# Splitting the weights of a two-block fp32 network with DMA transfers instead of VectorE

## The chip, the core and the metric

The kernel runs on one core of one Trainium2 chip. The metric is the device time of one execution in microseconds; the time before is the median of three runs. A profile comes from one further execution, whose own time stands beside its span below. The engines that matter are TensorE (PE in the profile, its weight loads PEld), VectorE (DVE), ScalarE (ACT), GpSimd (POOL) and SyncE (SP), which only issues transfers. Transfers can be issued from the queues of SP, ACT and POOL.

## The reference

Two transformer-like blocks run over 512 positions of width 1024, all in fp32, with one layer each.

```python
# first block
h = rmsnorm(x, attn_norm_g)
z = h @ w_in
gates = sigmoid(h @ w_gate + b_gate)
y_a, y_b, y_c = gmlp_mixer(...), pool_mixer(...), diff_attn_mixer(...)   # from columns of z
x = x + (g_a * (y_a @ proj_a) + g_b * (y_b @ proj_b) + g_c * (y_c @ proj_c)) @ w_out
x = x + conv_ffn(rmsnorm(x, ffn_norm_g), w_up, conv_w, conv_b, w_down)    # gelu(conv(gate)) * up
x = rmsnorm(x, final_norm_g)
# second block
x = x + dilated_attention_mixer(rms_norm(x, mixer_norm), attn_w_in, q_gain, k_gain, attn_w_out)
x = x + conv_ffn_2(rms_norm(x, ffn_norm), ffn_w_up, ffn_conv_w, ffn_conv_b, ffn_w_down)
```

`pool_mixer` takes moving averages over 2, 4, 8 and 16 positions. Both FFNs have 2816 hidden channels, that is 22 tiles of 128 for the gate and 22 for the up half.

## The kernel before

**Splitting.** TensorE multiplies operands of type float32r. To keep fp32 accuracy each operand is split in two: a leading part `hi`, the fp32 value rounded to float32r, and a remainder `lo`, the fp32 value less `hi`. A product is then three matmuls (`mm3`, line 97): hi·hi, hi·lo and lo·hi. This holds for activations (tiles xh and xl, ah and al, and so on) and for weights (tiles wh and wl).

**Units.** All weights pass through in 234 units (`unit`, line 151) of 128 partitions by 1024 columns, or 768 in every third unit of the two down projections. A unit is 24 matmuls of 128x512 (18 where it has 768 columns). The order is: uv (4 units), v (4), the q and k heads with the two units b0 and b1 of the pooling branch (10), the gates with the merging projections (32), the output projection `wo` (8), the first FFN's gate and up units in turn (44), its down projection `dn` (24); then the second block: q/k and v groups `n`, `vn`, `c` and `vc` (36), the output projection `wo2` (4), gate and up `vg` and `vu` (44) and the down projection `en` (24).

**A step.** The loop at line 1321 runs once for each unit, in an order written by hand; each engine executes its own instructions in program order. Step u consists of:

- `fn` (line 1323): the matmuls of unit u;
- `prep_hi(u+3)` (line 1324): ScalarE copies the loaded weights (tile wr) of unit u+3 to float32r, which makes wh;
- `prep_lo(u+2)` (line 1325): VectorE (POOL for the two units vg0 and vu0) subtracts wh from wr, which makes wl of unit u+2;
- the work that earlier steps put off (`early`);
- the loads of raw weights, issued from SP (`load`, line 161), up to six units ahead;
- `post`: the eviction of unit u's PSUM result and what follows from it; some of this is put off to a later step;
- `fills`: other work pinned to this step, such as attention scores, norms and transposes.

**Buffers.** wr has four buffers, wh four and wl three. The wl buffer of unit u+2 is that of unit u−1, so it is free once unit u−1's matmuls have ended; the same holds for the wh buffer of unit u+3.

**What POOL does.** The steps of the prediction touch these: `accumulate` (line 256) sums squares on POOL for a norm, once in each step m = 1 to 6 of the output projection (`wout_post`, line 710) and twice in each column m = 1 to 6 of the first down projection (`down1_post`, line 781). `rpow` (line 235) raises statistics to the power −0.5; it serves the norms (`r_a`, line 282; `b2_stat`, line 800), the attention (`da_n1`, line 605) and the q/k groups (`qk_norm`, line 845). `pool_win` (line 454) computes both tiles of the moving averages in the step of b1. `perm` (line 832) and `bd_prep` (line 874) copy and clear tiles at the start of the second block. In the FFNs one product of each pair of units runs on POOL (`gate1_post`, line 733, tile gl; `up2_post`, line 1150, tile act), put off to the step after its unit.

Of the kernel before, what the change touches and what calls it, by code (L numbers as in the profile page):

```python
# [23 lines left out]
F32 = mybir.dt.float32  # L24
F32R = mybir.dt.float32r
AF = mybir.ActivationFunctionType
OP = mybir.AluOpType
# [7 lines left out]
FT = 22  # L35
LA = 2
RAW = 4
WARM = 9
NSLOT = 51
NDUO = 13  # L40
# [15 lines left out]
def build(tc, a):  # L56
    nc = tc.nc
    te, ve, ac, po = nc.tensor, nc.vector, nc.scalar, nc.gpsimd
    ctx = ExitStack()
    with ctx:  # L60
        cp = ctx.enter_context(tc.tile_pool(name="cp", bufs=1))
        wp = ctx.enter_context(tc.tile_pool(name="wp", bufs=1))
# [22 lines left out]
        def f(t):  # L85
            return t.bitcast(F32)
# [15 lines left out]
        def tt(out, x, y, op, eng=None):  # L102
            (eng or ve).tensor_tensor(out, x, y, op=op)  # L103
# [41 lines left out]
        units = []  # L145
# [13 lines left out]
        raws, hls = {}, {}  # L159

        def load(j):
            if j < len(units):
                src, n = units[j][:2]
                raws[j] = wp.tile([128, 1024], F32, name="wr", tag="wr", bufs=RAW)
                nc.sync.dma_start(raws[j][:, :n], src)

        def prep_hi(j):
            if j < len(units):
                n = units[j][1]
                hi = wp.tile([128, 1024], F32R, name="wh", tag="wh", bufs=LA + 2)  # L170
                ac.activation(hi[:, :n], raws[j][:, :n], AF.Copy)  # L171
                hls[j] = hi

        def prep_lo(j):
            if j < len(units) and j in raws:
                n = units[j][1]
                lo = wp.tile([128, 1024], F32R, name="wl", tag="wl", bufs=LA + 1)
                tt(lo[:, :n], raws.pop(j)[:, :n], f(hls[j])[:, :n], OP.subtract,
                   po if names.get(j) in ON_POOL else ve)
                hls[j] = (hls[j], lo)  # L180

        def fm(out, hl, j0, n, xh, xl, k0, start, stop, t=slice(0, S)):
            hi, lo = hl
            for k in range(n):
                c = slice((j0 + k) * 128, (j0 + k + 1) * 128)
                mm3(out[:, t], hi[:, c], lo[:, c], xh[k0 + k][:, t], xl[k0 + k][:, t],
                    start and k == 0, stop and k == n - 1)
# [481 lines left out]
        for m2 in range(4):  # L669
# [6 lines left out]
            def fn(hl, m2=m2, st=st):  # L676
                for e in range(2):
                    pa, pb = acc(), acc()
                    st[e] = (pa, pb)
                    for t in range(2):  # L680
                        for y, p, o in ((YA, pa, 0), (YB, pb, 2)):
                            c = slice((4 * e + o + t) * 128, (4 * e + o + t + 1) * 128)
                            mm3(p, hl[0][:, c], hl[1][:, c], y[t][0], y[t][1], t == 0, t == 1)
# [570 lines left out]
        g0 = cp.tile([128, 8], F32, name="g0")  # L1254
        ve.memset(ones, 1.0)
        ac.activation(hb[:, :1], ones[:, :1], AF.Copy)
        raws[0] = wp.tile([128, 1024], F32, name="wr", tag="wr", bufs=RAW)
        for m in range(8):
            X[m] = slot("x")
        xs = lambda m: a["xT"][128 * m:128 * m + 128, :]  # L1260
# [6 lines left out]
        for m in (3, 5, 7):  # L1267
            nc.gpsimd.dma_start(X[m], xs(m))
        for j in range(1, RAW):
            nc.sync.dma_start(X[2 * j], xs(2 * j))  # L1270
            load(j)
            if j == 2:
                nc.sync.dma_start(prm, a["prm"])
        for i in range(WARM):
            te.matmul(warm[:, :128], ones, ones, start=True, stop=True)
        ve.memset(mh, -0.5)
        wh0 = wp.tile([128, 1024], F32R, name="wh", tag="wh", bufs=LA + 2)
        wl0 = wp.tile([128, 1024], F32R, name="wl", tag="wl", bufs=LA + 1)
        hls[0] = (wh0, wl0)
        XH[0], XL[0] = slot("xh", F32R), slot("xl", F32R)  # L1280
        p0.extend(misc() for _ in range(4))
# [15 lines left out]
        for j in range(1, LA + 1):  # L1297
            norm_in(2 * j, X[2 * j], g0[:, 2 * j:2 * j + 1], "r1")
            prep_hi(j)
            prep_lo(j)  # L1300
            norm_in(2 * j + 1, X[2 * j + 1], g0[:, 2 * j + 1:2 * j + 2], "r1")
# [17 lines left out]
        pend = []  # L1319
        loaded = RAW  # L1320
        for u_, (src, n, fn, post, defer) in enumerate(units):
            now[0] = u_
            fn(hls.pop(u_))
            prep_hi(u_ + LA + 1)
            prep_lo(u_ + LA)
            first = names.get(u_) in FIRST
            if not first:
                for fl, args in early.pop(u_, []):
                    fl(*args)
            while loaded <= u_ + LA + RAW and loaded < len(units):  # L1330
                load(loaded)
                loaded += 1
            if post is not None:
                pend.append((u_ + defer, post))
            while pend and pend[0][0] <= u_:
                pend.pop(0)[1]()
            if first:
                for fl, args in early.pop(u_, []):
                    fl(*args)
            for fl, args in fills.get(u_, []):  # L1340
                fl(*args)
        assert not pend and not early, early.keys()


# [115 lines left out]
```

## Time and profile before

| | |
|---|---|
| median of 3 runs | 1374.84 us (1374.4 to 1374.93) |
| the profiled execution's own time | 1375.68 us |
| its span, first to last instruction | 1373.8 us |
| mean granted TensorE clock | 0.999 |
| transfers | 46185 packets; 127.19 MB read from HBM |

How to read the lines that the prediction shows: in a row of the groups stand line, engine, operation, tiles written and read, shapes and count, then busy time in us and the mean of one in ns, then idle time of the engine just before them and what ended it. A row of the timeline begins with the start and the duration in us; in brackets stands how long the engine was idle before it and what released it. A row of the chain of work that ended last has the start, the length, and the engine, tile and line. A row of transfers has the issuing queue (SPq, POOLq), the count, the size of one, and the median time from its issue to its landing. A row of the windows has, for a stretch of time, the length and the busy time of PE, PEld, DVE, ACT and POOL with their instruction counts, then the granted clock, the share of time the DMA engines were busy, and GB/s.

### The profile page before, as it was taken

The page shows a single profiled execution, that of the slowest core. Times are in us where ns is not written, and L with a number is a line of the kernel's source. Part 1 is how long each engine was busy: PE and PEld are TensorE (multiplying, and loading weights), DVE is VectorE, ACT ScalarE, POOL GpSimd, SP SyncE. Part 2 cuts the span into 40 slices and gives each one's busy share as a digit, 9 for nine tenths or more (in the row PEclk, how much of TensorE's full clock was granted, in tenths as well). Part 3 has the DMA queues.
Part 4 walks back from the last instruction along what each step waited for, and adds up shares of the span by engine and source line. Part 5 has one row for each costly group of instructions (what it writes and reads, how often), then busy time and mean ns, then how long its engine had stood idle before and what let it go on. Part 6 is the DMA issues. An engine that isn't in the chain of part 4 may idle for free.

```text
span 1373.8 us, 16670 instructions
## 1 busy us (share of the span) xinstructions
PE 1363.8 (99%) x6360; PEld 1137.4 (83%) x6360; DVE 808.5 (59%) x1328; ACT 603.2 (44%) x974; POOL 248.7 (18%) x208
## 2 busy tenths in 40 slices
PE   9999999999999999999999999999989999999998
PEld 7888888888888888888888888888868888888887
DVE  6777664556555545533347667667878666665222
ACT  6547543333343333332234667645654444443110
POOL 3250111101111111101117122231341111110000
PEclk9999999999999999999999999999999999999999
DMA  7434222433333332333323342222123233223330
GB/s 256 127 101 124 77 79 90 129 116 92 106 95 92 96 104 92 91 97 100 96 92 98 104 109 63 69 85 63 62 88 97 93 93 106 93 88 107 115 110 25
DMA packets 46185, 134.62 MB, mean 98 GB/s; under 512 B 9924, under 2 KB 10639, under 8 KB 46105
## 3 DMA queue, kind: packets, MB, share of 16 engines
q1 hardware_dynamic: 45048, 131.30, 31.3%
q0 software_dynamic: 912, 2.19, 0.5%
q8 instruction: 50, 0.82, 0.2%
q14 instruction: 31, 0.25, 0.1%
q10 hardware_dynamic: 144, 0.07, 0.0%
HBM read 127.19 MB, written 2.14 MB: 94 GB/s over the span
## 4 chain that ended last, share of the span: by engine, by line
PE 98%; DVE 1%; issue 0%; ACT 0%; DMA 0%; DVEq 0%; POOLq 0%
PE acc L89 89%; PE ms L89 2%; PE cs L89 1%; PE cu L89 1%; PE qkt L885 1%; PE nu L89 1%; PE sc L89 1%; PE ns L89 1%; PE pv L89 1%; DVE xl L106 1%; PE ctr L1056 0%; PE ntr L949 0%; PE tr L583 0%; DVE y L103 0%; DMA g<-in_prm 0%
## 5 line engine op out<-in xcount | busy, mean ns | idle before, releaser
L89 PE MATMUL acc<-xh,wh 128*128 128x512 f32 x968 | 378.0, 390 | 0.0
L89 PE MATMUL acc<-xl,wh 128*128 128x512 f32 x968 | 376.8, 389 | 0.0
L89 PE MATMUL acc<-xh,wl 128*128 128x512 f32 x968 | 376.8, 389 | 0.0
L103 DVE TENSOR_TENSOR wl<-wr,wh 128x1024 fp32r<-128x1024 f32 (+2 forms) x233 | 297.3, 1276 | 127.7 <-PE acc L89 77.3
L171 ACT ACTIVATE wh<-wr 128x1024 fp32r<-128x1024 f32 (+1 forms) x233 | 242.0, 1039 | 210.9 <-PE acc L89 174.0
L89 PEld LDWEIGHTS acc<-xh,wl 128*128 128x128 f32 x968 | 181.7, 188 | 38.2
L89 PEld LDWEIGHTS acc<-xh,wh 128*128 128x128 f32 x968 | 181.7, 188 | 37.3
L89 PEld LDWEIGHTS acc<-xl,wh 128*128 128x128 f32 x968 | 181.8, 188 | 37.0
L89 PE MATMUL acc<-al,wh 128*128 128x512 f32 (+1 forms) x358 | 138.0, 385 | 0.0
L89 PE MATMUL acc<-ah,wl 128*128 128x512 f32 (+1 forms) x358 | 138.0, 385 | 0.0
L89 PE MATMUL acc<-ah,wh 128*128 128x512 f32 (+1 forms) x358 | 138.0, 385 | 0.0
L725 ACT ACTIVATE cv<-z,prm 128x512 f32<-128x512 f32 x66 | 53.7, 816 | 165.8 <-DVE z L103 165.8
L106 DVE SCALAR_TENSOR_TENSOR cv<-z,prm,cv 128x511 f32<-128x511 f32 (+1 forms) x132 | 99.5, 756 | 2.4
L89 PEld LDWEIGHTS acc<-al,wh 128*128 128x128 f32 x358 | 67.2, 188 | 13.6
L89 PEld LDWEIGHTS acc<-ah,wl 128*128 128x128 f32 x358 | 67.2, 188 | 13.5
L89 PEld LDWEIGHTS acc<-ah,wh 128*128 128x128 f32 x358 | 67.2, 188 | 13.4
L89 PE MATMUL acc<-wh,ch 128*128 128x512 f32 x192 | 75.8, 395 | 0.0
L89 PE MATMUL acc<-wl,ch 128*128 128x512 f32 x192 | 74.9, 390 | 0.0
L89 PE MATMUL acc<-wh,cl 128*128 128x512 f32 x192 | 74.8, 390 | 0.0
L103 POOL TENSOR_TENSOR gl<-cv,r2b 128x512 f32<-128x512 f32 x22 | 28.4, 1290 | 202.9 <-ACT cv L739 202.9
L103 POOL TENSOR_TENSOR act<-cv,cv 128x512 f32<-128x512 f32 x22 | 28.4, 1289 | 202.0 <-DVE cv L106 188.4
L236 POOL TENSOR_TENSOR rr<-ss,mh 128x8 f32<-128x8 f32 x24 | 38.8, 1644 | 114.1 <-DVE ss L857 114.1
(333 smaller groups left out, 1958.4 us busy)
## 6 DMA issues: line engine op xcount, KB each, us to landing
wr<-in_w_up SPq DMA_DIRECT2D x88, 512.0 KB, 3.5
wr<-in_w_dn SPq DMA_DIRECT2D x32, 512.0 KB, 3.5
wr<-in_w_g SPq DMA_DIRECT2D x24, 512.0 KB, 3.5
wr<-in_w_qkc SPq DMA_DIRECT2D x16, 512.0 KB, 3.5
wr<-in_w_o SPq DMA_DIRECT2D x12, 512.0 KB, 3.5
wr<-in_w_dn SPq DMA_DIRECT2D x16, 384.0 KB, 3.1
wr<-in_w_qkn SPq DMA_DIRECT2D x8, 512.0 KB, 3.9
wr<-in_w_vc SPq DMA_DIRECT2D x8, 512.0 KB, 3.4
```

The lines of the kernel that those rows point to most:

```text
L89: te.matmul(out, l, r, start=start, stop=stop, skip_group_check=True)
L103: (eng or ve).tensor_tensor(out, x, y, op=op)
L106: ve.scalar_tensor_tensor(out, x, s, y, op0=o0, op1=o1)
L171: ac.activation(hi[:, :n], raws[j][:, :n], AF.Copy)
L236: po.tensor_tensor(out, src, mh[:, :n], op=OP.pow)
L725: ac.activation(c, z, AF.Identity, scale=P(cw, 2 * n + j), bias=P(cb, j))
L885: te.transpose(p[:, 128 * b:128 * b + 128], qs[b][:, 128 * part:128 * part + 128], identf)
```

## The change

From index 12 of the units on (the thirteenth), no raw weights are loaded to SBUF any more. A transfer issued from POOL reads the fp32 weights from HBM and converts them to float32r as it writes wh (`cast`). ScalarE writes −wh to wl (`negate`). A second transfer from POOL reads the weights from HBM again and adds them to wl (`add`), so wl holds the weights less wh. In the loop the negation stands for unit u+2 where the VectorE subtraction stood; the add for unit u+2 and the cast for unit u+4 come at the very end of step u, behind its fills. wh has five buffers instead of four, wr three instead of four, wl three as before. The first twelve units are prepared as before.

```diff
+WH = 5
+WL = 3
+J0 = 12
         def load(j):
-            if j < len(units):
+            if j < min(J0, len(units)):
                 src, n = units[j][:2]
-                raws[j] = wp.tile([128, 1024], F32, name="wr", tag="wr", bufs=RAW)
+                raws[j] = wp.tile([128, 1024], F32, name="wr", tag="wr", bufs=3)
                 nc.sync.dma_start(raws[j][:, :n], src)
...
+        def cast(j):
+
+            if J0 <= j < len(units):
+                src, n = units[j][:2]
+                hi = wp.tile([128, 1024], F32R, name="wh", tag="wh", bufs=WH)
+                nc.gpsimd.dma_start(hi[:, :n], src)
+                hls[j] = hi
+
+        def negate(j):
+            if J0 <= j < len(units):
+                n = units[j][1]
+                lo = wp.tile([128, 1024], F32R, name="wl", tag="wl", bufs=WL)
+                ac.activation(lo[:, :n], f(hls[j])[:, :n], AF.Copy, scale=-1.0)
+                hls[j] = (hls[j], lo)
+
+        def add(j):
+
+            if J0 <= j < len(units):
+                src, n = units[j][:2]
+                nc.gpsimd.dma_start(hls[j][1][:, :n], src, accum_op=OP.add)
...
             fn(hls.pop(u_))
             prep_hi(u_ + LA + 1)
             prep_lo(u_ + LA)
+            negate(u_ + 2)
...
             for fl, args in fills.get(u_, []):
                 fl(*args)
+            add(u_ + 2)
+            cast(u_ + 4)
```

`prep_hi` and `prep_lo` get the same bound `min(J0, len(units))` as `load`, and all allocations of wh and wl use `WH` and `WL`.

More of the change, by code (lines that the diff above doesn't have):

```diff
@@ L161, in load @@
         def load(j):
-            if j < len(units):
+            if j < min(J0, len(units)):
                 src, n = units[j][:2]
-                raws[j] = wp.tile([128, 1024], F32, name="wr", tag="wr", bufs=RAW)
+                raws[j] = wp.tile([128, 1024], F32, name="wr", tag="wr", bufs=3)
                 nc.sync.dma_start(raws[j][:, :n], src)
         def prep_hi(j):
-            if j < len(units):
+            if j < min(J0, len(units)):
                 n = units[j][1]
-                hi = wp.tile([128, 1024], F32R, name="wh", tag="wh", bufs=LA + 2)
+                hi = wp.tile([128, 1024], F32R, name="wh", tag="wh", bufs=WH)
                 ac.activation(hi[:, :n], raws[j][:, :n], AF.Copy)
@@ L174, in prep_lo @@
         def prep_lo(j):
-            if j < len(units) and j in raws:
+            if j < min(J0, len(units)) and j in raws:
                 n = units[j][1]
-                lo = wp.tile([128, 1024], F32R, name="wl", tag="wl", bufs=LA + 1)
+                lo = wp.tile([128, 1024], F32R, name="wl", tag="wl", bufs=WL)
                 tt(lo[:, :n], raws.pop(j)[:, :n], f(hls[j])[:, :n], OP.subtract,
@@ L180, in prep_lo @@
                 hls[j] = (hls[j], lo)
+        def cast(j):
+            if J0 <= j < len(units):
+                src, n = units[j][:2]
+                hi = wp.tile([128, 1024], F32R, name="wh", tag="wh", bufs=WH)
+                nc.gpsimd.dma_start(hi[:, :n], src)
[3 more added lines that the diff above has]
+                n = units[j][1]
+                lo = wp.tile([128, 1024], F32R, name="wl", tag="wl", bufs=WL)
+                ac.activation(lo[:, :n], f(hls[j])[:, :n], AF.Copy, scale=-1.0)
[4 more added lines that the diff above has]
+                nc.gpsimd.dma_start(hls[j][1][:, :n], src, accum_op=OP.add)
         def fm(out, hl, j0, n, xh, xl, k0, start, stop, t=slice(0, S)):
@@ L1256, in build @@
         ac.activation(hb[:, :1], ones[:, :1], AF.Copy)
-        raws[0] = wp.tile([128, 1024], F32, name="wr", tag="wr", bufs=RAW)
+        raws[0] = wp.tile([128, 1024], F32, name="wr", tag="wr", bufs=3)
         for m in range(8):
@@ L1276, in build @@
         ve.memset(mh, -0.5)
-        wh0 = wp.tile([128, 1024], F32R, name="wh", tag="wh", bufs=LA + 2)
-        wl0 = wp.tile([128, 1024], F32R, name="wl", tag="wl", bufs=LA + 1)
+        wh0 = wp.tile([128, 1024], F32R, name="wh", tag="wh", bufs=WH)
+        wl0 = wp.tile([128, 1024], F32R, name="wl", tag="wl", bufs=WL)
         hls[0] = (wh0, wl0)
```

## The prediction

> **What bounds the kernel now.** I read first the page's busy shares and its chain, then the whole chain in order of time, then the POOL engine's timeline, since POOL receives the work.
>
> ```profile
> span 1373.8 us, 16670 instructions
> PE 1363.8 (99%) x6360; PEld 1137.4 (83%) x6360; DVE 808.5 (59%) x1328; ACT 603.2 (44%) x974; POOL 248.7 (18%) x208
> PE 98%; DVE 1%; issue 0%; ACT 0%; DMA 0%; DVEq 0%; POOLq 0%
> ...
> L103 DVE TENSOR_TENSOR wl<-wr,wh 128x1024 fp32r<-128x1024 f32 (+2 forms) x233 | 297.3, 1276 | 127.7 <-PE acc L89 77.3
> ```
>
> ```profile
> 5.93 24.02 PE ms L89 x96
> ...
> 252.98 108.84 PE acc L89 x480
> ...
> 368.19 353.63 PE acc L89 x1560
> ...
> 1026.91 342.99 PE acc L89 x1530
> ```
>
> TensorE sets the end. In the third long stretch 1560 matmuls take 353.63 us, 0.2267 us each, with no gap, so a unit of 24 matmuls lasts 5.44 us. The DVE subtraction that the change takes away (1.28 us in each unit) lies beside those 5.44 us and is nowhere in the chain. So there is next to nothing to win: the question is whether the two weight halves still arrive in time, for whatever is late now is added to a chain that has no slack.
>
> **What the change moves.** From index 12 on (222 of 234 units) one SP load, one ScalarE copy and one DVE subtraction become a POOL-issued cast, a ScalarE negation of the same size (costed as the copy: no change) and a POOL-issued add. SP loses 222 loads, DVE some 280 us that cost nothing before. POOL, 18% busy, gains 444 issues.
>
> ```profile
> wr<-in_w_up SPq DMA_DIRECT2D x88, 512.0 KB, 3.5
> ...
> wr<-in_w_dn SPq DMA_DIRECT2D x16, 384.0 KB, 3.1
> ...
> x<-in_xT SPq DMA_DIRECT2D x11, 256.0 KB, 3.8
> ...
> x<-in_xT POOLq DMA_DIRECT2D x4, 256.0 KB, 7.0
> ...
> msk<-in_msk POOLq DMA_DIRECT2D x1, 256.0 KB, 3.9
> ```
>
> ```profile
> 20.26 2.11 POOL L450 DMA_DIRECT2D pw<-in_pool_w  x4 [3.70 <-DVE pw L447]
> 22.33 0.58 POOL L495 DMA_DIRECT2D oh<-in_oh  x1
> ```
>
> An issue takes POOL 0.53 to 0.58 us (2.11 over 4; 0.58), so 444 make some 245 us: POOL goes to about 36%, harmless as a share. The order is what matters. The last two rows show that POOL issues strictly in turn: oh depends on nothing, yet it goes out only after pw, which stood waiting for DVE.
>
> The price of one add, from issue to landing, is not in this trace. Its lower bound is a plain load of the same size, 3.5 us. Its upper bound is the dearest POOL-issued 256 KB, 7.0 us, in the crowded first microseconds. Between: 512 KB against 384 KB differ by 0.4 us, so a pass over 512 KB costs 1.6 us; an add also reads what it adds to, a second pass, 3.5 + 1.6 = 5.1; POOL's 256 KB took 0.1 more than SP's. I take 5.2 us and keep 3.5 and 7.0 for the range.
>
> The step's order decides the rest. In step u the add for unit u+2 stands at the very end, behind every POOL instruction of that step. The DVE subtraction stood ahead of them, on another engine. So where a POOL instruction of step u waits for unit u's own matmuls, the add for u+2 is issued only after unit u has ended, with one unit (5.44 us) left instead of two. The added wait is (end of the last POOL instruction of step u) + 5.2 − (start of unit u+2 before).
>
> The new waits themselves are short. The add waits for ScalarE's negation, which can start when unit u−1 has ended, as the copy did; behind it on POOL stand the cast for u+4 and the next step's sums and powers, whose users (ScalarE, DVE, the statistics) have a step or more of slack. The negation waits for its cast, issued two steps earlier right behind an add; behind it on ScalarE stand the step's evictions. Each lead is about two units, 10.9 us, less the delays below, and I cost both at nothing; if a cast came later than that, the evictions would be next, and then TensorE's PSUM banks.
>
> Down projection of the first FFN: x2, then norm, squares, and two POOL sums.
>
> ```profile
> 626.66 0.69 DVE L103 TENSOR_TENSOR x<-acc,x 128x512 f32<-128x512 f32 x1 [2.80 <-PE acc L89]
> ```
>
> ```profile
> 628.71 1.34 POOL L103 TENSOR_TENSOR rfacc<-sq 128x512 f32<-128x512 f32 x1 [31.99 <-ACT sq L279]
> 630.02 2.00 POOL L103 TENSOR_TENSOR rgacc<-sq 128x512 f32<-128x512 f32 x1
> ```
>
> The unit ended about 0.2 us before x, at 626.5, so the unit after next starts at 631.9. POOL is free at 632.0; the add lands at 637.2: 5.3 us late, in six of the eight columns: 31.8 us.
>
> Output projection: one POOL sum in steps 1 to 6 of eight.
>
> ```profile
> 325.83 1.33 POOL L103 TENSOR_TENSOR r2acc<-sq 128x512 f32<-128x512 f32 x1 [75.64 <-ACT sq L279]
> ```
>
> Free at 327.16; the unit after next would start at 252.98 + 14 × 5.442 = 329.17: 3.2 us late. Once it is late the next add has that time to spare, so every second one stalls: 3 × 3.2 = 9.6 us.
>
> The pooling windows (step of b1), which put over twenty POOL instructions in one step:
>
> ```profile
> 84.96 1.04 POOL L103 TENSOR_TENSOR wsum<-zb 128x511 f32<-128x511 f32 x1 [37.61 <-DVE zb L103]
> ...
> 104.49 1.30 POOL L103 TENSOR_TENSOR pd<-win,zb 128x512 f32<-128x512 f32 x1
> ```
>
> ```profile
> 97.12 5.44 PE acc L89 x24
> ```
>
> Free at 105.79, unit due at 97.12: 13.9 us late. Next the start of the second block, where the statistics and the permuting copies stand on POOL (with the memsets and four powers ahead of the second copy):
>
> ```profile
> 727.21 1.09 POOL L835 CAST cl<-xl 128x512 fp32r<-128x512 f32 x1
> ...
> 750.11 1.59 POOL L835 CAST cl<-xl 128x512 fp32r<-128x512 f32 x1
> ```
>
> ```profile
> 722.81 10.91 PE acc L89 x48
> ...
> 734.15 16.35 PE acc L89 x72
> ```
>
> Free at 728.30, due at 722.81 + 5.46 = 728.27: 5.2 us. Free at 751.70, due at 734.15 + 10.90 = 745.05: 11.9 us (both move alike with what came before).
>
> Powers on POOL behind the statistics of a step's own result: four in the attention, five after the q/k groups, one each behind the second and third norm; the first and last of the two groups, and the two single ones, with the units they delay:
>
> ```profile
> 164.40 1.03 POOL L236 TENSOR_TENSOR or<-om,mh 128x4 f32<-128x4 f32 x1 [14.73 <-DVE om L608]
> ...
> 243.09 1.86 POOL L236 TENSOR_TENSOR or<-om,mh 128x4 f32<-128x4 f32 x1 [22.75 <-DVE om L608]
> ...
> 363.53 1.92 POOL L236 TENSOR_TENSOR r<-ms,mh 128x4 f32<-128x4 f32 x1 [9.16 <-DVE ms L285]
> ```
>
> ```profile
> 793.88 6.44 POOL L236 TENSOR_TENSOR rr<-ss,mh 128x8 f32<-128x8 f32 x4 [31.83 <-DVE ss L857]
> ...
> 942.89 6.44 POOL L236 TENSOR_TENSOR rr<-ss,mh 128x8 f32<-128x8 f32 x4 [22.37 <-DVE ss L857]
> ...
> 1022.25 1.93 POOL L236 TENSOR_TENSOR r<-ms,mh 128x4 f32<-128x4 f32 x1 [8.55 <-DVE ms L285]
> ```
>
> ```profile
> 169.92 5.46 PE acc L89 x24
> ...
> 241.63 10.92 PE acc L89 x48
> ...
> 797.43 10.91 PE acc L89 x48
> ...
> 950.84 5.47 PE acc L89 x24
> ```
>
> Attention: 165.43 + 5.2 − 169.92 = 0.7 for the first, 244.95 + 5.2 − 247.09 = 3.1 for the last; with the two between, 9.6 us for the four. Groups: 800.32 + 5.2 − 802.89 = 2.6 and 949.33 + 5.2 − 950.84 = 3.7; 14.1 for the five. The norms: 365.45 + 5.2 − 368.19 = 2.5, and 1024.18 + 5.2 − 1026.91 = 2.5.
>
> The 88 up-projection units nearly escape, as their POOL product belongs to the step before:
>
> ```profile
> 508.40 1.28 POOL L103 TENSOR_TENSOR gl<-cv,r2b 128x512 f32<-128x512 f32 x1 [9.65 <-ACT cv L739]
> ...
> 1122.90 1.29 POOL L103 TENSOR_TENSOR act<-cv,cv 128x512 f32<-128x512 f32 x1 [9.59 <-DVE cv L106]
> ```
>
> 509.68 + 5.2 = 514.9 against a due time of 368.19 + 27 × 5.442 = 515.1, and 1124.19 + 5.2 = 1129.4 against 1026.91 + 19 × 5.442 = 1130.3. No cost, but 0.2 and 0.9 us are all the cover: every tenth that an add takes over 5.4 us costs 2.2 us in the first FFN's 22 pairs.
>
> Waits: 31.8 + 9.6 + 13.9 + 5.2 + 11.9 + 9.6 + 14.1 + 2.5 + 2.5 = 101 us.
>
> **The clock** comes on top.
>
> ```profile
> 1370.00:1374.00 4.00, 0.00 (x0) 0.00 (x0) 0.35 (x1) 0.00 (x0) 0.00 (x0) 0.74 0.10 35
> ```
>
> In the last 4 us TensorE has nothing to do and the granted clock averages 0.74: half speed for some 2 of the 4, after some 2 of idling. A cold start costs 24.02 − 96 × 0.2267 = 2.3 us in the first chain row. Ten of the waits above pass 4.5 us (six columns, the pooling, the two at the second block, one group): 10 × 2.2 = 22 us. The Trainium skill, "TensorE: Matmul & The Clock Gate", section "What's actually happening", has the clock halve after an idle window of about 3.4 us and return after as long a busy one; by it each restart would cost about 1.7 us, 17 in all, and the trace's quicker fall at the end disagrees with its idle time.
>
> Costed at nothing: the third weight buffer instead of a fourth in the first units (the fourth load waits for the first buffer; cover is ScalarE's squares, and the range holds the rest). Sum: 1375.68 us (the profiled execution: 1373.8 of span and 1.9 around it, 0.8 above the median 1374.84) + 123; against the median, **1498 us**.
>
> **Rivals.** (1) *A cheap add.* If it lands like a plain load (3.5), each of 22 waits is 1.7 us shorter and most stay too short to cool the clock: 123 − 37 − 15 = 71, 1446 us. It is also the time if the converting transfer doesn't round at all: the copies are the same. (2) *A dear add, or transfers at their limit.*
>
> ```profile
> 258.00:722.00 464.00, 464.00 (x2051) 384.15 (x2050) 234.56 (x275) 168.35 (x214) 57.84 (x41) 1.00 0.33 100
> ```
>
> A plain load now keeps the DMA engines busy for 0.33 × 5.44 = 1.8 us a unit, the small ones included; about 1.7 is the load. Cast and add at three passes need 5.1 of 5.44 and fit; at four, 6.8 don't: 1.3 us more in each of the 148 units of the two gapless stretches, 192 us, 1690. An add of 7.0 us that is only late gives 1.8 × 22 + (1.6 + 0.9) × 22 = 95 more, 1593. The Trainium skill, "Collectives: The Full Stack", section "The bandwidth ceiling: the fold count and why AG ≠ RS ≠ AR", says a transfer that adds is slower for its two reads and not for the addition; by it add and cast would be three passes. No row here shows one. (3) *Not slower.* If POOL took the adds past its waiting instructions, every add would have two units, 10.9 us, and even 7.0 us would be hidden; the relief of DVE and the 1% of idle TensorE then allow at most some 5 us of gain, 1370. It decides where POOL's queue isn't in order; the pw and oh rows speak against it.
>
> **How the numbers follow.** Forecast (adds of 4.4 to 6 us, 1470 to 1560): 0.52. Cheap add: 0.15. Dear add or transfer limit: 0.30. Not slower: 0.03. Range 1440 to 1690: from the cheap add to the transfer limit, leaving out what is beyond four passes and the last rival. A measurement of this kernel can tell about 0.2%: faster by more 0.02, within 0.01, slower 0.97.
>
> **What would show it.** Right: TensorE waits for wl's DMA, none in the up-projections, about 5 us at every third unit of the first down projection, over 10 at the pooling and the second block; none in the last down projection, whose steps have no POOL work. Granted clock under 1 after those. Landing of an add about 5 us. Wrong: waits in every unit, DMA share near 1 (the limit); POOL issues of adds ahead of its sums; landings far from 5 us; or a wait for wh instead of wl, a cast that comes late.

## The result, and the profile after

The changed kernel takes 1518.84 us (median of 4 runs, 1513.77 to 1522.02) against 1374.88 us before: ratio 1.1044, 95% interval 1.1019 to 1.1069, so 144 us slower. The forecast was 1498 us in a range of 1440 to 1690. The profiled execution has a span of 1519.0 us at a mean granted clock of 0.966.

From the page of the changed kernel: span, busy times, share of the chain by engine, three groups, the POOL queue's packets, and the two kinds of transfer.

```profile
span 1519.0 us, 16761 instructions
...
PE 1408.4 (93%) x6360; PEld 1162.2 (77%) x6360; DVE 544.5 (36%) x1108; ACT 605.0 (40%) x974; POOL 538.8 (35%) x650
...
q0 software_dynamic: 64848, 230.81, 66.5%
...
PE 37%; DMA 5%; issue 4%; POOL 2%; DVE 2%; ACT 2%; POOLq 0%; DVEq 0%; ACTq 0%
...
L197 ACT ACTIVATE wl<-wh 128x1024 fp32r<-128x1024 f32 (+1 forms) x222 | 230.8, 1040 | 403.2 <-PE acc L92 129.6
...
L92 PE MATMUL acc<-ah,wl 128*128 128x512 f32 (+1 forms) x358 | 143.3, 400 | 25.5 <-DMA wl<-in_w_dn 25.5
...
L204 POOL DMA_DIRECT2D wl<-in_w_up x88 | 77.4, 880 | 76.2 <-ACT wl L197 74.3
...
wh<-in_w_up POOLq DMA_DIRECT2D x88, 512.0 KB, 6.9
wl<-in_w_up POOLq DMA_DIRECT2D x88, 512.0 KB, 5.6
```

TensorE is busy for 93% in place of 99%, and its own busy time has grown by 45 us (1363.8 to 1408.4) with the same 6360 matmuls: time was lost both by waiting and by slower matmuls. VectorE got 264 us freer, which bought nothing. The last two rows are the new prices: 5.6 us for an add, 6.9 for a cast, which stands behind an add.

Who kept TensorE waiting is in its list of waits (us in total, times, longest):

```profile
PE acc L92 <- DMA wl<-in_w_dn: 25.5, 6, 4.4
PE acc L92 <- DMA wl<-in_w_up: 10.9, 7, 3.1
PE acc L92 <- DMA wl<-in_w_vn: 10.8, 1, 10.8
PE acc L92 <- DMA wl<-in_w_k: 10.7, 1, 10.7
PE acc L92 <- DMA wl<-in_w_qkc: 9.9, 4, 4.6
PE acc L92 <- DMA wl<-in_w_qkn: 8.7, 2, 4.4
PE acc L92 <- DMA wl<-in_w_o: 8.6, 3, 2.9
PE acc L92 <- DMA wl<-in_w_g: 7.8, 5, 2.8
PE ms L92 <- DMA wl<-in_w_up: 5.8, 1, 5.8
```

Every large wait is for an add (wl), none for a cast (wh). One column of the first down projection, from the timeline of the changed kernel (start, duration, engine; in brackets the idle time and what ended it):

```profile
672.27 0.69 DVE L106 TENSOR_TENSOR x<-acc,x 128x512 f32<-128x512 f32 x1 [12.73 <-PE acc L92]
674.32 1.33 POOL L106 TENSOR_TENSOR rfacc<-sq 128x512 f32<-128x512 f32 x1 [8.79 <-ACT sq L303]
675.62 1.29 POOL L106 TENSOR_TENSOR rgacc<-sq 128x512 f32<-128x512 f32 x1
676.85 0.86 POOL L204 DMA_DIRECT2D wl<-in_w_dn  x1
677.42 0.84 POOL L190 DMA_DIRECT2D wh<-in_w_dn  x1
...
682.20 0.50 PE L92 MATMUL acc<-ah,wl 128*128 128x512 f32 x1 [4.07 <-DMA wl<-in_w_dn]
```

The add goes out as soon as the second sum leaves POOL, and lands 5.3 us later; TensorE had then been out of work for 4.1 us.

The slower matmuls are seen in the windows of the changed kernel (length; busy PE, PEld, DVE, ACT, POOL; granted clock; DMA share; GB/s): the first down projection, and two microseconds just behind the wait above.

```profile
670.00:800.00 130.00, 104.50 (x407) 83.53 (x406) 8.66 (x12) 28.28 (x36) 42.15 (x50) 0.91 0.61 136
684.00:686.00 2.00, 2.00 (x6) 1.62 (x5) 0.00 (x0) 1.06 (x1) 0.32 (x1) 0.50 1.09 289
```

The starts of all 6360 matmuls can be compared one by one in both traces. The last one starts 145.6 us later than before: 108.1 us are single delays of over 0.6 us (the waits), 41.6 us are smaller ones of over 0.1 us, and 4.1 us were won back elsewhere. Of the 41.6 us, 38.0 lie in the stretches of half clock or at their edges; 3.6 lie outside them.

### The profile page after: what moved, and what is told of

Read it like the earlier page. It is cut to its first block, busy times and chain, and to the rows that moved or that the text cites. A ratio compares the mean times of both kernels' runs of the same rounds, so it can differ in the third digit from the quotient of the medians.

```text
span 1519.0 us, 16761 instructions
## 1 busy us (share of the span) xinstructions
PE 1408.4 (93%) x6360; PEld 1162.2 (77%) x6360; DVE 544.5 (36%) x1108; ACT 605.0 (40%) x974; POOL 538.8 (35%) x650
## 3 DMA queue, kind: packets, MB, share of 16 engines
q0 software_dynamic: 64848, 230.81, 66.5%
## 4 chain that ended last, share of the span: by engine, by line
PE 37%; DMA 5%; issue 4%; POOL 2%; DVE 2%; ACT 2%; POOLq 0%; DVEq 0%; ACTq 0%
PE acc L92 34%; DMA wl<-in_w_qkc 1%; DMA wl<-in_w_dn 1%; POOL rr L260 1%; DMA wl<-in_w_qkn 1%; PE cu L92 1%; DMA wl<-in_w_up 1%; PE qkt L909 1%; PE nu L92 0%; PE ns L92 0%; DVE cv L109 0%; PE cs L92 0%; DMA wl<-in_w_vn 0%; DMA wl<-in_w_vc 0%; ACT wl L197 0%
## 5 line engine op out<-in xcount | busy, mean ns | idle before, releaser
L92 PE MATMUL acc<-xh,wl 128*128 128x512 f32 x968 | 381.4, 394 | 29.3 <-DMA wl<-in_w_up 10.9
L197 ACT ACTIVATE wl<-wh 128x1024 fp32r<-128x1024 f32 (+1 forms) x222 | 230.8, 1040 | 403.2 <-PE acc L92 129.6
L92 PE MATMUL acc<-ah,wl 128*128 128x512 f32 (+1 forms) x358 | 143.3, 400 | 25.5 <-DMA wl<-in_w_dn 25.5
L92 PE MATMUL acc<-ah,wh 128*128 128x512 f32 (+1 forms) x358 | 142.6, 398 | 0.0
L92 PE MATMUL acc<-al,wh 128*128 128x512 f32 (+1 forms) x358 | 142.2, 397 | 0.0
L204 POOL DMA_DIRECT2D wl<-in_w_up x88 | 77.4, 880 | 76.2 <-ACT wl L197 74.3
L92 PE MATMUL acc<-wl,ch 128*128 128x512 f32 x192 | 78.3, 408 | 13.5 <-DMA wl<-in_w_qkc 9.9
L204 POOL DMA_DIRECT2D wl<-in_w_dn x48 | 43.6, 908 | 121.6 <-ACT wl L197 104.3
L190 POOL DMA_DIRECT2D wh<-in_w_up x88 | 77.0, 875 | 0.0
```

Source lines behind the costliest of these rows:

```text
L92: te.matmul(out, l, r, start=start, stop=stop, skip_group_check=True)
L190: nc.gpsimd.dma_start(hi[:, :n], src)
L197: ac.activation(lo[:, :n], f(hls[j])[:, :n], AF.Copy, scale=-1.0)
L204: nc.gpsimd.dma_start(hls[j][1][:, :n], src, accum_op=OP.add)
```

## Experiments

The theory: TensorE waits because the add for unit u+2 stands on POOL behind step u's own sums, powers and copies; a landing of 5.6 us does the rest, and the clock falls behind the waits. Rivals: the two POOL transfers are dear or near the DMA engines' limit wherever they stand; or it is the cast that comes late.

**1. Same transfers, issued early.**

```diff
             negate(u_ + 2)
+            add(u_ + 2)
+            cast(u_ + 4)
...
-            add(u_ + 2)
-            cast(u_ + 4)
```

> The add for unit u+2 and the cast for u+4 are issued right behind the negation, ahead of the step's put-off work, post and fills; nothing else changes. Theory A (the adds stand behind POOL work that waits for the same step's matmuls): the waits at wo, dn, the q/k groups and the norms go; what is left is the second add behind the pooling windows (105.8 + 5.6 - 102.8, some 9 us) and the one behind the permuting copies (about 6), with two cold restarts: 1390 to 1405 us. Theory B (an add costs its 5.6 us wherever it stands, or the transfers are at their limit): nothing moves by more than some 20 us, 1495 to 1520.

Measured: 1391.59 us, ratio 1.0114 (1.0099 to 1.0129). The landing of an add is the same 5.6 us, and yet 127 of the 144 us are gone. TensorE's list of waits in this run has only two for wl left:

```profile
PE acc L92 <- DMA wl<-in_w_q: 8.1, 1, 8.1
PE acc L92 <- DMA wl<-in_w_vn: 4.6, 1, 4.6
```

These come where POOL is still busy with the step before when the add comes up. The POOL timeline of this run at the pooling windows:

```profile
102.31 1.27 POOL L106 TENSOR_TENSOR pd<-win,zb 128x512 f32<-128x512 f32 x1
103.52 0.92 POOL L204 DMA_DIRECT2D wl<-in_w_q  x1
```

The queue is in order as before; the add of step 14 (for q3) now stands behind the pooling of step 13.

**2. Only the cast early.**

```diff
             negate(u_ + 2)
+            cast(u_ + 4)
...
             add(u_ + 2)
-            cast(u_ + 4)
```

> Only the converting transfer for unit u + 4 is issued at the head of step u, behind the negation; the adding transfer for u + 2 stays at the step's end, behind POOL's sums. Theory (the adding transfer's place behind POOL's own work makes the waits; the converting one, issued two units sooner, has slack): the waits for wl stay, 1500 to 1525 us, within 1.5% of the changed kernel's 1518.8. Rival (it is the converting transfer's place, by making the negation late): near the run with both issued early, 1390 to 1410 us. If the queue's order counts too (the add then stands behind one transfer more), up to 1535 us.

Measured: 1520.96 us, ratio 1.1053 (1.1032 to 1.1073): the changed kernel again. The waits are the same too, as the first two rows of TensorE's list show:

```profile
PE acc L92 <- DMA wl<-in_w_dn: 26.7, 6, 4.6
PE acc L92 <- DMA wl<-in_w_up: 11.1, 7, 3.1
```

So it is the add's place, and the cast's place at the step's end costs nothing there.

**3. The second transfer without the addition.** It overwrites wl with the weights, so the remainder is not computed; reads, issues and order stay.

```diff
-                nc.gpsimd.dma_start(hls[j][1][:, :n], src, accum_op=OP.add)
+                nc.gpsimd.dma_start(hls[j][1][:, :n], src)
```

> The second transfer writes the weights over wl instead of adding them (a cast like the first; wl then holds the whole weight, the output is not the reference's). All waits and orders stay. Theory A with the second pass as the add's price: its packets fall from 0.33 to 0.17 us per 4 KB, its landing from 5.6 to some 4.2 us, so each of some 25 waits is 1.4 us shorter and some cold restarts go: 1465 to 1490 us. Rival (the landing is POOL's issue and a fixed latency, adding costs nothing): landing and time stay, 1510 to 1522.

Measured: 1456.84 us, ratio 1.0591 (1.0570 to 1.0612): 62 us less, somewhat below the expected range. Transfers of this run:

```profile
q0 software_dynamic: 64848, 230.81, 50.1%
...
wh<-in_w_up POOLq DMA_DIRECT2D x88, 512.0 KB, 4.6
wl<-in_w_up POOLq DMA_DIRECT2D x88, 512.0 KB, 3.8
```

The same packets and bytes take 50.1% of 1456.3 us in place of 66.5% of 1519.0: over 16 engines and 64848 packets 180 ns a packet, against 249 as a mean of casts and adds, so an adding packet takes about 2 × 249 − 180 = 318 ns (an estimate; the median packets of 4 KB in the changed kernel's trace are 174 ns for a cast and 328 for an add). The add's extra landing time, 1.8 us, paid once in each of some 22 waits makes 40 us. The comparison of starts agrees: the waits fall by 42 us (108.1 to 66.1) and the smaller delays by 19 (41.6 to 22.1), with ten falls of the clock in place of twenty. More than half of the loss is still there: the place comes first, the price second.

**4. The sums of two stages moved off POOL.** In the output and first down projections VectorE adds the squares.

```diff
-            square(m, x1, "r2")
+            square(m, x1, "r2", eng=ve)
...
-            square(m, x2, "rf")
-            square(m, x2, "rg", scale=P("final_g", m))
+            square(m, x2, "rf", eng=ve)
+            square(m, x2, "rg", scale=P("final_g", m), eng=ve)
```

> The sums of squares of the output projection and of the first down projection go from POOL to VectorE; order and transfers stay. Theory A: those nine places (6 at dn with 38.0 us, 3 at wo with 15.3 us, cold restarts included) lose their wait, as POOL has nothing left there that waits for the step's own unit; all other places stay: 1519 - 53 = 1466, between 1460 and 1475. Rival (it is the add's or the transfers' price there, since every unit moves three passes): the nine waits stay, 1510 to 1522.

Measured: 1464.36 us, ratio 1.0644 (1.0626 to 1.0662). All nine waits of these two stages are gone and the large ones elsewhere stay: 18 sums, 22 us of POOL's busy time (538.8 to 517.2), cost 54 us in their place on POOL.

**5. The clock alone.** Fourteen matmuls that compute nothing keep TensorE busy ahead of the six late columns.

```diff
+KEEP = tuple(f"dn{m}_1" for m in range(2, 8))
...
+            if names.get(u_) in KEEP:
+                d = misc("dummy")
+                for i in range(14):
+                    mm(d, onesr, AH[0], True, True)
```

> Ahead of the six waiting units of the first down projection (dn2_1 to dn7_1) 14 matmuls of 128x512 into an unused PSUM tile are put, 3.2 us of work in a wait of 4.2 to 4.6 us; they add nothing to the result. Theory C (a wait lets the granted clock fall to half, and the first 3.4 us after it run at half speed): the clock stays at 1.0 there, each of the six places falls from 6.0-7.2 to about 4.4 us above its 5.44, 10 us in all: 1506 to 1512. Rival (the slower matmuls come from the transfers, or the clock falls for another reason): the slow matmuls stay and the time is 1516 to 1525.

Measured: 1510.77 us, ratio 1.0981 (1.0962 to 1.0999). In the window of that stage the clock is 1.00 in place of 0.91:

```profile
670.00:800.00 130.00, 122.65 (x529) 98.39 (x528) 12.61 (x18) 33.37 (x43) 42.28 (x50) 1.00 0.67 149
```

The six places shrink from 38.0 to about 29 us though the adds land no sooner: that much of their cost was the clock.

**6. The cast alone.** VectorE subtracts as before the change, the raw weights come over SP's queue for all units; no negation, no add.

```diff
         def load(j):
-            if j < min(J0, len(units)):
+            if j < len(units):
...
-            if j < min(J0, len(units)) and j in raws:
+            if j < len(units) and j in raws:
...
-            negate(u_ + 2)
...
-            add(u_ + 2)
             cast(u_ + 4)
```

> The leading part comes from the converting transfer on POOL's queue, at the end of the step and four units ahead; the raw weights still come over SP's queue and VectorE still subtracts; no negation and no adding transfer. Theory (the converting transfer costs nothing in its place, and neither do its bytes): 1373 to 1382 us, same as before, with ScalarE some 230 us freer. Rival (the converting transfer is late behind POOL's sums too, or two transfers for each unit crowd the DMA engines): waits for wh or for wl appear, over 1390 us.

Measured: 1406.02 us, ratio 1.0216 (1.0201 to 1.0232). The theory missed: the run is 30 us slower than before. The largest place, 13.6 us at vn_1 with the slower matmuls behind its wait, is a cast that comes late. First the largest row of TensorE's waits, then VectorE and POOL in the timeline at the second block:

```profile
PE qkt L909 <- DVE qr L106: 12.8, 6, 10.8
```

```profile
764.57 0.59 POOL L190 DMA_DIRECT2D wh<-in_w_vn  x1
...
768.56 3.93 DVE L106 TENSOR_TENSOR wl<-wr,wh 128x1024 fp32r<-128x1024 f32 x1 [11.32 <-issue]
...
772.42 3.37 DVE L106 TENSOR_TENSOR qr<-qr,rr 128x512 f32<-128x512 f32 x4
```

The cast goes out late behind POOL's copies, as the adds do, and lands at 768.48. VectorE, in order too, stands 11.3 us before its subtraction, which reads wh, and the norm of q behind it, which doesn't read it, is late for TensorE. Behind the pooling windows it is the same, with VectorE late for the attention scores; that place costs 8.6 us:

```profile
112.83 1.22 DVE L106 TENSOR_TENSOR wl<-wr,wh 128x1024 fp32r<-128x1024 f32 x1 [6.91 <-DMA wh<-in_w_k]
```

A late transfer thus delays whatever stands behind its first reader. The other 9 us of this run lie in smaller places and were not traced to a cast.

**7. One unit more of lead.** All three steps early, negation and add for u+3, a fourth wl buffer; one 512-column slot and one buffer of the wider temporaries are given up for the room.

```diff
-WL = 3
+WL = 4
...
-NSLOT = 51
+NSLOT = 50
...
-            return tp.tile([128, w], F32, name=name, tag=f"t{w}", bufs=6 if w < 64 else 2)
+            return tp.tile([128, w], F32, name=name, tag=f"t{w}", bufs=6 if w < 64 else 1)
...
-            negate(u_ + 2)
+            cast(u_ + 4)
+            negate(u_ + 3)
+            add(u_ + 3)
...
-            add(u_ + 2)
-            cast(u_ + 4)
```

> At the head of step u: the converting transfer for u + 4, the negation for u + 3, the adding transfer for u + 3, with a fourth buffer for wl (one slot of 512 columns and a second temporary buffer are given up for its room). Theory (what the early issue left, 8.1 us at q3 and 4.6 us at vn_0, is lateness of the one add behind a POOL that was busy when it came up, and one unit more of 5.4 us takes up most of it): 1375 to 1382 us. Rival (the rest is the DMA engines' limit, or the adding transfer is dear in itself): no better than the 1391.6 us of the early issue, 1386 to 1395 us. The slot given up may cost some us at the end of attention in either case.

Measured: 1391.94 us, ratio 1.0115 (1.0102 to 1.0129), no better than experiment 1. The wait at q3 is gone and 2.1 us at k3 are left of it, but others have come, as two rows of TensorE's waits and two of ScalarE in the timeline show:

```profile
PE acc L92 <- ACT qr L878: 3.7, 1, 3.7
PE ns L92 <- DMA dbl<-dbl: 3.6, 1, 3.6
```

```profile
735.42 1.06 ACT L197 ACTIVATE wl<-wh 128x1024 fp32r<-128x1024 f32 x1 [7.83 <-DMA wh<-in_w_vn]
...
744.48 1.06 ACT L197 ACTIVATE wl<-wh 128x1024 fp32r<-128x1024 f32 x1 [6.82 <-DMA wh<-in_w_vn]
```

The negation, moved a unit nearer to its cast, now makes ScalarE stand for 7 us with the eviction qr behind it. The cast that the second row waits for went out at 735.52, behind POOL's copies, and took 8.9 us to land. The wait went from POOL's queue to ScalarE's. How much the buffers given up added was not separated.

**8. Four passes over the weights.** Experiment 1, and all raw weights also go over SP's queue into buffers that nothing reads.

```diff
         def load(j):
-            if j < min(J0, len(units)):
+            if j < len(units):
```

> The early issue, and beside it every unit's weights once more over SP's queue into the raw buffers, which nothing reads from unit 13 on: four passes over the weights in place of three. Theory (the DMA engines are near their limit: 128 packets a unit at 159 + 174 + 328 ns over 16 engines are 5.3 us, with some 0.6 us of other traffic 5.9 us against the 5.44 us of a unit's matmuls): about 0.45 us on each of some 160 units, 70 us, so 1430 to 1480 us and a DMA share over 0.95. Rival (a share of 0.85 hides more room than it shows, as packets waiting for memory lie beside each other): 1388 to 1400 us.

Measured: 1445.78 us, ratio 1.0505 (1.0490 to 1.0519), in the theory's range, but not spread as expected. As nothing reads these buffers, SP runs ahead of the units: in 300 to 530 us it issues 75 loads beside 36 casts and 36 adds. The same window of experiment 1 and of this run:

```profile
300.00:530.00 230.00, 230.00 (x1018) 190.44 (x1017) 76.24 (x116) 88.01 (x113) 88.47 (x106) 1.00 0.85 193
```

```profile
300.00:530.00 230.00, 205.12 (x859) 157.92 (x859) 63.01 (x97) 74.22 (x94) 74.57 (x90) 1.00 1.06 328
```

At a DMA share of 0.85 TensorE is never idle; at 1.06 it loses 25 of 230 us, and most units there last 6.4 us in place of 5.44. The packets add up to that. Each transfer is 8 packets of 4 KB an engine, at the median times of 159 ns for a plain load (kernel before), 174 for a cast and 328 for an add (changed kernel): 8 × (75 × 159 + 36 × 174 + 36 × 328 ns) = 240 us of work in 230 us. In this window the packets themselves took hardly longer (medians of 173, 174 and 327 ns), so it was the engines that were full. Their time is a real limit, and the early issue stays under it by 15% here.

**9. The new path without its two bad places.** Experiment 1, with units 15 to 20 and 127 to 134 prepared as before the change.

```diff
-J0 = 12
+OLD = set(range(12)) | set(range(14, 20)) | set(range(126, 134))
...
-            if j < min(J0, len(units)):
+            if j in OLD:
...
-            if J0 <= j < len(units):
+            if j < len(units) and j not in OLD:
```

> The early issue from unit 13 on, but units 15 to 20 (pooling) and 127 to 134 (the second block's first two projections) are made as before the change, by ScalarE and VectorE. Theory (what the early issue left sits only where POOL is busy when the add comes up, and nothing else of the new path costs time): 1371 to 1377 us, within 0.2% of before. Rival (the wait moves to the first unit behind each gap, whose transfers are issued into the same busy stretch): 1380 to 1392 us.

Measured: 1374.94 us, ratio 0.9992 (0.9983 to 1.0001). 208 units go by cast, negation and add, and it costs nothing that can be measured.

**10. Only from unit 135 on**, early issue. **11. Only from unit 163 on**, early issue. **12. The kernel before with three raw buffers** in place of four.

```diff
-J0 = 12
+J0 = 134
```

> Early issue as in the first experiment, but the new path only from unit 135 on; the units of pooling, projections and attention's q are made as before the change. Theory (the transfers cost nothing where POOL's queue is free ahead of them, and VectorE's relief is worth about 1 us at the first gated unit): 1371 to 1376 us, within 0.2% of before. Rival (the three transfers of a unit slow the units they lie beside): over 1380 us.

```diff
-J0 = 12
+J0 = 162
```

> As the late start, but the new path only from unit 163 on (the second attention's output projection and the second feed-forward). Theory (the late start's gain is VectorE's relief at the first gated unit of the second feed-forward, 1.37 us in the profile): 1371.5 to 1374.5 us, the same gain. Rival (the gain comes from VectorE's relief in the second block's attention): no gain, 1375 to 1376 us.

```diff
-                raws[j] = wp.tile([128, 1024], F32, name="wr", tag="wr", bufs=RAW)
+                raws[j] = wp.tile([128, 1024], F32, name="wr", tag="wr", bufs=3)
```

> The kernel before with three buffers for raw weights in place of four, and nothing else. Theory (the shorter first unit, 1.2 to 1.7 us less in every later profile, is where the clock's window falls, not an effect of the buffers): 1374 to 1376 us, same as before. Rival (fewer loads crowd the first ones, so the first unit really is shorter): 1373 to 1374 us, and part of the late start's gain is this.

Measured: 1372.41 us, ratio 0.9975 (0.9965 to 0.9985); 1373.00 us, 0.9981 (0.9972 to 0.9990); 1374.72 us, 0.9993 (0.9984 to 1.0003). The first two beat the kernel before, by about 0.2%. Their profiles are about 1.4 us shorter than before at the first gated unit of the second feed-forward (vg0). The third is not shorter there, so the gain doesn't come from the three raw buffers. But experiment 9 has the same 1.4 us there and loses it again in others, so this gain is about as small as what can be told. The 0.6 us between the first two lie within their intervals.

## Why the prediction was right, and where its sizes were off

**TensorE bounds it and VectorE's relief is worth nothing**: right. VectorE fell from 808.5 to 544.5 us; the only gain found anywhere is the 1.4 us at vg0.

**POOL issues in order, the add behind the step's work**: right, shown by experiments 1, 2 and 4. The third rival (adds taken past waiting work) fell with them.

**The price of an add, 5.2 us**: 5.6 by the page, 5.3 in the column shown. A second pass on top of the load was the right model: without the addition the same transfer lands in 3.8 us, so the pass is 1.8 us (estimate: 1.6). That pass took 62 us out of the kernel where the first rival's sum had 37 + 15.

**The waits, 101 us**: 108.1 us, but as a sum of errors both ways. By place, in the gaps between matmuls: six columns 26.5 (predicted 31.8), output projection 9.1 (9.6), pooling 10.8 (13.9), n0_2 4.5 (5.2), vn_1 11.0 (11.9), four q/k groups 13.9 (14.1 for five), attention powers 8.7 over five units (9.6 for four), the unit behind the second norm (ug1) 1.3 (2.5), the one behind the third (vu1) 1.2 (2.5). These were too high by 14 us, of which 7 are a POOL that became faster: rgacc took 2.00 us before and 1.29 after (six times), and the pooling windows on POOL shrank from 20.8 to 18.0 us from first to last instruction (83.64 to 101.66). Here the prediction moved POOL's rows over unchanged, although the subtraction beside them was to go. Too low was the list of places: vg0 (5.9), n0_3 (4.6), ug3 and uu3 (4.8) and vg3 (3.3) stand nowhere in it; 2.7 us are two small gaps elsewhere. At vg0 the trace shows POOL's sums r3acc ahead of the add, up to 1139.35 us, which no term of the prediction has.

**No cost in the up-projections, with 0.2 and 0.9 us of cover**: right but for the starts of both stages (ug1, ug3, uu3, vg0, vu1, vg3); of the rest only one unit waited over 0.6 us (1.0).

**New waits of the cast and the negation at nothing**: right for the changed kernel (experiment 2), but only in that arrangement. Where VectorE reads the cast (experiment 6) or the negation stands nearer to it (experiment 7), the cast is late, issued behind POOL's work (in experiment 7 it is also slow to land, 8.9 us), and blocks another queue.

**The clock, 22 us**: this is the term that was mis-sized: 38 us, shown by experiment 5 for one stage. The price of a fall was nearly right (38 over 20 falls is 1.9 us; 2.2 predicted); the count was not. The step took only waits above 4.5 us, ten of them, and the clock fell twenty times: behind all waits of 3.7 us or more, and behind seven of twelve between 1.6 and 3.3 us (the last section shows what told these apart).

**The transfer limit** (5.1 of 5.44 us at three passes): right, with 0.85 measured where 0.94 was worked out, and experiment 8 shows that crossing it would have cost in nearly every unit, as the second rival said (about 0.9 us each, where it had 1.3).

The sum came out 21 us low: 16 us from the clock, 3.6 from the small delays outside its stretches, which had no term, and 7 from the waits, less 4 won back elsewhere; the rest is the distance between the profiled executions and the medians. That the waits came within 7 us of the forecast is partly luck, as errors of 14 and 21 us cancelled.

## What to carry to other kernels

A transfer issued from a compute engine's queue (here POOL's) starts when the work ahead of it on that engine is done; price its landing from there, and put the issue ahead of any instruction that waits for the current unit's result. The same holds for the first reader of the transfer: what stands behind it on its engine is late with it. Moving work off an engine that is not the bound won next to nothing here: the arrangements that hid it all came back to the time before, or 0.2% below it.

## What the runs showed of the hardware that was not expected

**The clock falls in steps, and the phase of a wait counts.** The half-clock stretches of the changed kernel are 3.413, 6.827 or 10.24 us long, 30 times 3.413 in all. A wait of 1.8 us was enough once (timeline of the changed kernel; matmuls of 0.39 us become 0.63):

```profile
210.80 0.51 PE L92 MATMUL acc<-xh,wl 128*128 128x512 f32 x1 [1.80 <-DMA wl<-in_w_g]
...
212.07 0.39 PE L92 MATMUL acc<-xl,wh 128*128 128x512 f32 x1
212.30 0.59 PE L92 MATMUL acc<-xh,wl 128*128 128x512 f32 x1
212.69 0.63 PE L92 MATMUL acc<-xh,wh 128*128 128x512 f32 x1
```

while one of 2.8 us that ended at 268.14 left the clock alone. The phase decides. All half-clock stretches of the trace start on one grid of 3.413 us (at 99.70, 212.34 and 355.70, for example, 33 and 42 steps apart). As far as the profile's matmul ends go, each of the twenty falls came behind a step of this grid in which TensorE had idled 1.80 us or more; from 12 us on, no step at full clock with over 1.84 us of idling was without a fall. The traces of experiments 2 to 5 have their border at about 1.9 us. The wait before 268.14 is cut by the grid into 1.65 and 1.19 us. In these five traces, then, somewhat over half a step of idling was enough.

The Trainium skill, "TensorE: Matmul & The Clock Gate", section "What's actually happening", gives a free-running window of about 3.4 us; the step of 3.413 us agrees, but its rule that the clock falls after an idle window of that length does not: seven shorter waits brought it down.

**Some instructions of POOL and VectorE slow each other.** In the kernel before, VectorE's subtraction of 128x768 took 0.95 us alone and 2.06 beside POOL's sums of 128x512, and rgacc took 2.00 us beside it and 1.29 without it. Not every pair does: beside POOL's powers the subtraction of 128x1024 kept its 1.22 us. In the timeline of experiment 11 the same VectorE instruction took 0.75 us alone and 1.75 us beside POOL's sums:

```profile
1006.77 0.75 DVE L109 SCALAR_TENSOR_TENSOR xl<-y,prm,xh 128x512 fp32r<-128x512 f32 x1 [0.19 <-ACT xh L298]
1007.65 4.98 POOL L106 TENSOR_TENSOR r3acc<-r3acc,sq 128x512 f32<-128x512 f32 x3
1008.04 1.75 DVE L109 SCALAR_TENSOR_TENSOR xl<-y,prm,xh 128x512 fp32r<-128x512 f32 x1
```

**An issue on POOL is shown longer than it holds the queue**: 0.86 us in the column of the first section, but two that follow each other start 0.57 us apart (676.85 and 677.42).
